# Seven of a layer's seventeen input chunks as seven block products, in a two-layer decoder trunk

## The chip, the cores and the metric

One core of a Trainium2 chip runs the whole program. The metric is the device time of one execution in microseconds (us), lower is better. The engines are PE (TensorE, matrix products), DVE (VectorE), ACT (ScalarE), POOL (GpSimd) and SP, whose queue starts the transfers. Each works through its own instructions in the order in which the program was built, and waits for others at semaphores.

## The reference

Two layers on x of 256 tokens by 2048 features, fp32. Each layer normalises, projects 2048 features to 8200 columns (q, k, v and gate of four mixers A to D of 8 heads each, and 8 forget logits), runs four kinds of causal attention, gates, projects back and adds to x:

```python
h = rms_norm(x, norm_gain[layer])
proj = jnp.einsum('bsd,dc->bsc', h, w_in[layer])       # 2048 -> 8200
qkv = proj[..., :3 * MIX_WIDTH].reshape(bsz, seq, 3, N_MIXERS, N_HEADS_PER_MIXER, HEAD_DIM)
gate = proj[..., 3 * MIX_WIDTH:4 * MIX_WIDTH]
log_f = jax.nn.log_sigmoid(proj[..., 4 * MIX_WIDTH:] + forget_bias[layer])
# A dilated windows, C block sparse, D forget-gated: softmax; B stick-breaking; A, C, D with QK-norm
y = jnp.stack([o_a, o_b, o_c, o_d], axis=1) ...
x = x + jnp.einsum('bsc,cd->bsd', y * jax.nn.silu(gate), w_out[layer])
```

## The kernel before

**Products.** Every fp32 projection is three products of a rounded format: high part by high part, high by low, low by high. The activations are split once a layer (`xh`, `xl`), the weights as they stream: a transfer on SP's queue brings `raw`, ACT copies it to the rounded `wh`, DVE subtracts to get `wl = raw - wh`, both inputs in SBUF, and PE multiplies.

**Units.** A layer has 17 input chunks of 512 columns (`IN_ORDER`, in the order qA vA kA qC vC kC, half of qD, gA, other half of qD, gC vD kD qB kB vB gD gB) and 4 output chunks. A chunk has four row blocks s of 512 features, 1 MB each, and a row block four tiles of 128 features. A unit is two such tiles, 128 x 1024 elements of weight, and `split(u + 2)` is issued just before `unit(u)`. Chunks in *token form* (q, v, k of A, C, D, and vB) hold a block of x still in PE and move 512 columns of weight past it: 96 matmuls of 512 a chunk. The others (the gates, qB, kB, and the output chunks) hold weight and move 256 tokens: 192 matmuls of 256.

**Order.** The program is built by a planner that keeps a clock for every engine from cost formulas (`Engine.cost`); each side task (evacuation of a chunk, rotary products, an attention pair of heads) is a generator that goes on when the planned clocks say its inputs are there and a buffer is free (`pe(...)`, `vs(...)`, `run_tasks`). What comes out is one fixed order for each engine. At most two pairs of heads are open at a time. A pair runs `t` (transposes of q and k), ACT's copy `qt`, `s` (scores), DVE's mask and maximum, ACT's exponentials, a scaling by 1/sum on DVE, `pt` (transposes), two copies `ptb` (one ACT, one DVE), `o`, and ACT's copy. GpSimd does the rotary products of q and k, the gains, D's mask terms, and in layer 1 the sum of squares.

**Buffers.** Three `wh`, three `wl`, three `raw` of a whole row block, five `tmp`, and two each of q, k, v, p, qt, pt and o. In PSUM four banks are for attention (`att`) and four for projections (`proj`), two to a chunk. The residual x stays in SBUF (`xt`), and so do the split outputs `yh`, `yl` of the attention. An output chunk takes its four row blocks in the order of `OUT_MIX`, A, C, D, B.

Of the kernel before, what the change touches and what calls it, by code (L numbers as in the profile page):

```python
# [11 lines left out]
F32 = mybir.dt.float32  # L12
# [5 lines left out]
P = 128  # L18
# [27 lines left out]
OUT_MIX = [A, C, D, B]  # L46
# [8 lines left out]
def units_of_layer():  # L55

    units = []
    two = [(0, 1), (2, 3)]
    for c in range(len(IN_ORDER)):
        for s in range(4):  # L60
            units += [(c, s, h) for h in ([(0, 1, 2, 3)] if halved(c) else two)]
# [47 lines left out]
class Engine:  # L109
# [39 lines left out]
    def cost(self, op, out, aps, args, kw):  # L149
# [3 lines left out]
        if self.name == "T":  # L153
# [5 lines left out]
            return max(n, 256) * 0.000425 if not four else n * 0.00169 * four  # L159
        if self.name == "S":  # L160
            return (0.19 if "accum_out" in kw else 0.1) + n * 0.00083
        if self.name == "G":
            return 0.05 + n * 0.0023
        if op == "reduce_sum":
            n = max(a.free_size() for a in aps)
        return 0.07 + n * (0.00052 if op in ("tensor_scalar_mul", "tensor_scalar") else 0.00104)
# [3 lines left out]
def hybrid_kernel(ctx, tc, x_tr, w_all, w_half, gain, qk_gain, f_bias, rope, masks, out):  # L170
# [10 lines left out]
    ATT, WB, WARM = 4, 3, 4  # L181
# [7 lines left out]
    rings["proj"] = (proj, [None] * 4)  # L189
# [4 lines left out]

    ROWS, ROW_OF = [], []
    for l, c, s, h in UNITS:
        if h[0] == 0:
            ROWS.append((l, c, s))
        ROW_OF.append(len(ROWS) - 1)

    raw, wh, wl = {}, {}, {}

    def load_raw(i):
        if i >= len(ROWS):
            return
        l, c, s = ROWS[i]
        t = new("raw", (P, 4, HW if halved(c) else CW), f"raw{i}")
        if halved(c):
            Q.dma_start(t, w_half[l, IN_ORDER[c][2], s])
            raw[i] = t  # L210
            return
        c -= sum(halved(k) for k in range(c))
        if i == 0:
            for h in range(4):
                Q.dma_start(t[:, h, :], w_all[l, c, s, :, h, :])
                if h < 2:
                    Q.dma_start(xt[0][:, h, :], x_tr[0, :, h, :])
                if h == 0:
                    Q.dma_start(gain_sb, gain)
        elif i < 3:  # L220
            for h in range(2):
# [705 lines left out]
```

## Time and profile before

| | |
|---|---|
| time, median of 3 runs | 1030.92 us (1024.12 to 1031.61) |
| profiled execution | 1027.18 us, of which its span 1025.4 us |
| mean granted clock of PE, share of full speed | 0.997 |
| busy: PE, DVE, ACT, POOL | 1006.3, 649.3, 512.2, 174.1 us |
| PE matmuls | 6772, of them 1728 of 512 columns |
| moved by DMA | 176.62 MB |

The busy time of an engine is the time in which one of its instructions ran; matmuls overlap, so that the distance from one start to the next, not the duration of one, is what a matmul costs. Times in the views count from the start of the span. In the names, what stands before the arrow is written and what stands behind it is read; an entry in square brackets is the idle time of the engine before an instruction and who ended it.

### The profile page before, as it was taken

Reading aid. Unit: us, or ns where it says so; the run is one execution under the profiler, and the core shown is the slowest. Engines: PE = TensorE matmul, PEld = TensorE weight load, DVE = VectorE, ACT = ScalarE, POOL = GpSimd, SP = SyncE. Lnnn points to the kernel's source line nnn. Section 1 sums busy time; section 2 is a strip of 40 time slices with the busy share of each in tenths; the row PEclk is TensorE's granted clock in tenths of the full one; section 3 lists DMA queues with packets and bytes.
Section 4 is the critical chain, followed back from the end, with each engine's and each line's share of the span. In section 5 each row is a group of like instructions: output and inputs, shape, how many; then the busy total and the mean of one; then the engine's idle time right before and its main releaser. Section 6 shows DMA issues by size and latency. Waiting matters only on the chain. (4 is left out here: it accounts for less than half of the span.)

```text
span 1025.4 us, 16643 instructions
## 1 busy us (share of the span) xinstructions
PE 1006.3 (98%) x6772; PEld 895.0 (87%) x6772; DVE 649.3 (63%) x1064; ACT 512.2 (50%) x791; POOL 174.1 (17%) x154
## 2 busy tenths in 40 slices
PE   8999999999998999999999999999999989999998
PEld 6887779998798899999988877899988987999998
DVE  6856757676555656757677556586765565667543
ACT  6543554656453454545454435546474444554432
POOL 0244404000045200001116044040000631000000
PEclk9999999999999999999999999999999999999999
DMA  9654435526535444555555544344465454444462
GB/s 330 235 176 165 163 121 186 179 90 217 194 125 207 162 128 160 171 197 172 201 180 203 178 151 165 123 167 166 137 225 173 145 185 158 156 144 161 165 246 83
DMA packets 30189, 176.62 MB, mean 172 GB/s; under 512 B 3984, under 2 KB 4896, under 8 KB 11040
## 3 DMA queue, kind: packets, MB, share of 16 engines
q1 hardware_dynamic: 30112, 175.55, 49.9%
q8 instruction: 53, 0.87, 0.3%
q14 instruction: 24, 0.20, 0.1%
HBM read 173.42 MB, written 2.11 MB: 171 GB/s over the span
## 5 line engine op out<-in xcount | busy, mean ns | idle before, releaser
L119 DVE TENSOR_TENSOR wl<-raw,wh 128x1024 fp32r<-128x1024 f32 (+2 forms) x321 | 411.1, 1286 | 309.4 <-ACT wh L119 307.3
L119 ACT ACTIVATE wh<-raw 128x1024 fp32r<-128x1024 f32 (+2 forms) x321 | 337.9, 1055 | 399.3 <-PE pj L119 363.1
L119 PE MATMUL pj<-wh,xh 128*128 128x512 f32 (+1 forms) x704 | 269.2, 382 | 0.5 <-ACT xh L119 0.5
L119 PE MATMUL pj<-wl,xh 128*128 128x512 f32 (+1 forms) x704 | 264.3, 375 | 1.3 <-DVE wl L119 1.3
L119 PE MATMUL pj<-wh,xl 128*128 128x512 f32 (+1 forms) x704 | 263.3, 374 | 0.0
L119 PE MATMUL pj<-xh,wl 128*128 128x256 f32 x768 | 216.8, 282 | 6.2 <-DVE wl L119 6.2
L119 PE MATMUL pj<-xh,wh 128*128 128x256 f32 x768 | 220.6, 287 | 0.0
L119 PE MATMUL pj<-xl,wh 128*128 128x256 f32 x768 | 216.5, 282 | 0.0
L119 PEld LDWEIGHTS pj<-wh,xh 128*128 128x128 f32 x704 | 132.5, 188 | 29.6 <-issue 3.4
L119 PEld LDWEIGHTS pj<-wh,xl 128*128 128x128 f32 x704 | 132.6, 188 | 26.2 <-DVE xl L119 0.2
L119 PEld LDWEIGHTS pj<-wl,xh 128*128 128x128 f32 x704 | 132.9, 189 | 25.5 <-DVE wl L119 2.4
L119 PEld LDWEIGHTS pj<-xh,wh 128*128 128x128 f32 x768 | 145.3, 189 | 8.2 <-issue 8.0
L119 PEld LDWEIGHTS pj<-xh,wl 128*128 128x128 f32 x768 | 145.4, 189 | 6.6 <-DVE wl L119 6.6
L119 PEld LDWEIGHTS pj<-xl,wh 128*128 128x128 f32 x768 | 145.2, 189 | 0.2
L119 PE MATMUL pj<-yh,wl 128*128 128x256 f32 x512 | 144.0, 281 | 0.0
L119 PE MATMUL pj<-yh,wh 128*128 128x256 f32 x512 | 143.9, 281 | 0.0
L119 PE MATMUL pj<-yl,wh 128*128 128x256 f32 x512 | 143.9, 281 | 0.0
L119 PEld LDWEIGHTS pj<-yh,wh 128*128 128x128 f32 x512 | 96.3, 188 | 0.7 <-issue 0.7
L119 PEld LDWEIGHTS pj<-yh,wl 128*128 128x128 f32 x512 | 96.5, 188 | 0.0
L119 PEld LDWEIGHTS pj<-yl,wh 128*128 128x128 f32 x512 | 96.2, 188 | 0.0
L119 ACT ACTIVATE p<-p,mx 128x128 f32<-128x128 f32 x96 | 42.2, 442 | 1.7 <-DVE mx L119 1.7
L119 POOL TENSOR_TENSOR acc<-acc,xsq 128x512 f32<-128x512 f32 x7 | 9.4, 1338 | 172.2 <-ACT xsq L119 172.0
(112 smaller groups left out, 774.9 us busy)
## 6 DMA issues: line engine op xcount, KB each, us to landing
raw<-in_w_all_dram SPq DMA_DIRECT2D x149, 1024.0 KB, 4.9
raw<-in_w_half_dram SPq DMA_DIRECT2D x16, 520.0 KB, 3.5
raw<-in_w_all_dram SPq DMA_DIRECT2D x4, 512.0 KB, 8.0
nb<-rows SPq DMA_DIRECT2D x8, 256.0 KB, 5.1
xt<-in_x_tr_dram SPq DMA_DIRECT2D x7, 256.0 KB, 7.7
out_dram<-xt SPq DMA_DIRECT2D x6, 256.0 KB, 2.2
raw<-in_w_all_dram SPq DMA_DIRECT2D x4, 256.0 KB, 3.3
mask_sb<-in_masks_dram SPq DMA_DIRECT2D x1, 512.0 KB
```

Source lines behind the costliest of these rows:

```text
L119: r = f(*args, **kw)
```

## The change

Seven chunks of a layer, q, k and v of A, k and v of D, k and v of C, are computed by Strassen's scheme in its form with seven products: tokens, features and columns are each cut in two (128 tokens, two feature tiles, 256 columns), and seven products of blocks, four banks of PSUM to a chunk, take the place of eight. Three parts are added for it. `token_forms` makes sums and differences of token blocks on GpSimd and splits them into `fh`, `fl` (ACT, DVE), once a layer. `differences` makes, for each row block of such a chunk, sums and differences of weight blocks: `da` (128 x 1024) in one GpSimd instruction and `db` in two of 128 x 512. `evac_fast` puts the products together with one ACT copy and seven DVE additions of 256 elements out of PSUM. A row block of such a chunk is four *fast units* x = 0 to 3 of 12, 12, 12 and 6 matmuls of 256 columns: x = 0 takes the left half of the raw weights, 1 and 2 the differences, and 3 a quarter of the raw ones; each has its own `wh` and `wl` (1024, 1024, 1024 and 512 elements).

The order becomes qB kB vB gB qD (both halves) gA gD qC gC, ordinary, and then the seven fast ones; of the ordinary units ten come first, then in each fast chunk four ordinary ones and after every four fast units one more, and the six left over come last. `OUT_MIX` is B, A, D, C.

To make room x leaves SBUF: layer 0 writes its new x to DRAM (`xd`, 8 writes of 256 KB), and each layer reads x back before its output chunks (`reload`, 8 reads of 256 KB a layer) into the four `xT` buffers that the differences used. `yh`, `yl` and the token forms share a ring of eight (`ys`), and a y is made only after the last fast unit (flag `dead`). PSUM is two `att` and six `proj`; there is one qt and one pt, and `raw` holds half a row block. The scaling by 1/sum and the second `ptb` copy go from DVE to ACT, layer 0's sum of squares from DVE to GpSimd, and the planner's cost formulas get other constants. ACT loads a function table 48 times in the built program, where it was 12.

```diff
 IN_ORDER = [
-    ("q", A, None), ("v", A, None), ("k", A, None),
-    ("q", C, None), ("v", C, None), ("k", C, None),
-    ("q", D, 0), ("g", A, None), ("q", D, 1), ("g", C, None), ("v", D, None), ("k", D, None),
-    ("q", B, None), ("k", B, None), ("v", B, None),
-    ("g", D, None), ("g", B, None),
+    ("q", B, None), ("k", B, None), ("v", B, None), ("g", B, None), ("q", D, 0), ("q", D, 1), ("g", A, None),
+    ("g", D, None), ("q", C, None), ("g", C, None),
+    ("q", A, None), ("k", A, None), ("v", A, None), ("k", D, None), ("v", D, None), ("k", C, None), ("v", C, None),
 ]
+FAST = 10
...
-OUT_MIX = [A, C, D, B]
+OUT_MIX = [B, A, D, C]
...
+    slow = [(c, s, h) for c in range(FAST) for s in range(4) for h in ([(0, 1, 2, 3)] if halved(c) else two)]
+    fast = [(c, s, x) for c in range(FAST, len(IN_ORDER)) for s in range(4) for x in range(4)]
+    units, slow = slow[:10], slow[10:]
+    for c in range(FAST, len(IN_ORDER)):
+        units, slow = units + slow[:4], slow[4:]
         for s in range(4):
-            units += [(c, s, h) for h in ([(0, 1, 2, 3)] if halved(c) else two)]
+            units, fast = units + fast[:4] + slow[:1], fast[4:]
+            slow = slow[1:]
+    units += slow
...
-    ATT, WB, WARM = 4, 3, 4
+    ATT, PROJ, WB, WARM = 2, 6, 3, 4
...
-    slots = dict(q=2, k=2, v=2, tmp=5, gs=4, qt=2, nb=1, p=2, be=1, pt=2, o=2, wh=WB, wl=WB, raw=3)
+    slots = dict(q=2, k=2, v=2, tmp=6, gs=4, qt=1, p=2, be=1, pt=1, o=4, wh=WB, wl=WB, raw=3, rows=2, xT=4, ys=8)
...
+            t = raw[l, c, s] = new("rows", (P, 4, CW), f"rows{u}")
+            Q.dma_start(t, w_all[l, w, s])
+            spawn(differences(l, c, s), True)
...
+    def differences(l, c, s):
+        r = raw[l, c, s]
+        yield gp(r, xT=1)
+        a = dif[l, c, s, 1] = new("xT", (P, 4, SEQ), f"da{l}_{c}_{s}")
+        av = a.rearrange("p (n j) k -> p n j k", n=2)
+        G.tensor_sub(av, r[:, :, SEQ:].rearrange("p (n j) k -> p n j k", n=2),
+                     r[:, 0:2, :].rearrange("p j (n k) -> p n j k", n=2))
+        yield gp(r, xT=1)
+        b = dif[l, c, s, 2] = new("xT", (P, 4, SEQ), f"db{l}_{c}_{s}")
+        G.tensor_sub(b[:, 0:2, :], r[:, 2:4, SEQ:], a[:, 0:2, :])
+        G.tensor_sub(b[:, 2:4, :], r[:, 2:4, 0:SEQ], b[:, 0:2, :])
...
+        G.tensor_add(g1[:, :, t1], g0[:, :, t1], g1[:, :, t1])
+        G.tensor_sub(g0[:, :, t1], g0[:, :, t0], g0[:, :, t1])
+        G.tensor_sub(g0[:, :, t0], g1[:, :, t1], g0[:, :, t0])
+        G.tensor_sub(g1[:, :, t0], g1[:, :, t0], g0[:, :, t0])
...
-        (V if l == 0 else G).tensor_add(rr["acc"], rr["acc"], sq)
...
+            G.tensor_add(rr["acc"], rr["acc"], sq)
...
+        S.activation(p1, ps[0][:, lo], AF.Copy)
+        V.tensor_add(x[:, 0, lo], ps[0][:, hi], p1)
+        V.tensor_add(t[:, 0, :], ps[2][:, lo], p1)
+        V.tensor_add(t[:, 1, :], ps[1][:, hi], t[:, 0, :])
+        V.tensor_add(x[:, 1, lo], ps[2][:, hi], t[:, 1, :])
+        V.tensor_add(x[:, 1, hi], ps[1][:, lo], t[:, 1, :])
+        V.tensor_add(t[:, 0, :], ps[1][:, lo], t[:, 0, :])
+        V.tensor_add(x[:, 0, hi], ps[3][:, lo], t[:, 0, :])
+        done(*ps, t, p1)
...
+            V.tensor_mul(o[:, 2 * b:2 * b + 2, :], gs[b], o[:, 2 * b:2 * b + 2, :])
             done(gs[b])
+        yield vs(o, ys=2)
+        yield lambda: (l, "dead") in flags and room(1e9, ys=2)
+        a = new("ys", (P, 4, SEQ), f"yh{l}{m}", F32R)
+        b = new("ys", (P, 4, SEQ), f"yl{l}{m}", F32R)
+        S.activation(a, o, AF.Copy)
+        V.tensor_sub(b, o, a)
...
-                    V.tensor_scalar_mul(p[:, i, a:b], p[:, i, a:b], de[:, 2 * i + t:2 * i + t + 1])
+                    S.activation(p[:, i, a:b], p[:, i, a:b], AF.Copy, scale=de[:, 2 * i + t:2 * i + t + 1])
...
-        V.tensor_copy(pt[:, 1, :], pt_ps[1][:, 0:384])
+        S.activation(pt[:, 1, :], pt_ps[1][:, 0:384], AF.Copy)
...
+            yield lambda: (l, "dif") in flags and room(0.0, xT=1)
+            xt[c] = new("xT", (P, 4, SEQ), f"xr{l}{c}")
+            xuses[c] = 4
+            for b in range(2):
+                Q.dma_start(xt[c][:, 2 * b:2 * b + 2, :], (x_tr if l == 0 else xd)[2 * c + b])
...
+            Q.dma_start(xd[k], xt[c][:, 2 * b:2 * b + 2, :])
...
+        for n in range(1 if x == 3 else 2):
+            o = ps[x][:, n * SEQ:(n + 1) * SEQ]
+            run_tasks()
+            for j in range(2):
+                hi, lo = {(0, 0): tok(j, t0), (0, 1): tok(2 + j, t0), (1, 0): form(2 + j, t1), (1, 1): form(j, t1),
+                          (2, 0): form(j, t0), (2, 1): tok(2 + j, t1), (3, 0): form(2 + j, t0)}[x, n]
+                w = 2 * n + j
+                first = s == 0 and j == 0 and n == 0
+                T.matmul(o, lhsT=hi, rhs=a[:, w, :], start=first, stop=False, skip_group_check=True)
+                T.matmul(o, lhsT=hi, rhs=b[:, w, :], start=False, stop=False, skip_group_check=True)
+                T.matmul(o, lhsT=lo, rhs=a[:, w, :], start=False, stop=s == 3 and j == 1, skip_group_check=True)
...
+            if s == 3:
+                flags.add((l, "dead"))
...
+        fetch(u + 16)
```

On PE, the first rows of the third chunk in the program before, which is kA of layer 0, `pj0_2`; matrix moved first behind the arrow, then what is held:

```order
L119 MATMUL pj0_2_0_577<-wh16_532,xh0_94 128x512
L119 MATMUL pj0_2_0_577<-wl16_533,xh0_94 128x512
L119 MATMUL pj0_2_0_577<-wh16_532,xl0_110 128x512
L119 MATMUL pj0_2_1_578<-wh16_532,xh0_94 128x512
L119 MATMUL pj0_2_1_578<-wl16_533,xh0_94 128x512
L119 MATMUL pj0_2_1_578<-wh16_532,xl0_110 128x512
```

The same chunk of the changed program, `pj0_11`, first unit and the start of its third, which takes a difference `da` as its weights (`wh40`) and the token form `fh00`:

```order
L126 MATMUL pj0_11_0_1194<-wh38_1145,xh0_86 128x256
L126 MATMUL pj0_11_0_1194<-wl38_1146,xh0_86 128x256
L126 MATMUL pj0_11_0_1194<-wh38_1145,xl0_94 128x256
L126 MATMUL pj0_11_0_1194<-wh38_1145,xh0_86 128x256
L126 MATMUL pj0_11_0_1194<-wl38_1146,xh0_86 128x256
L126 MATMUL pj0_11_0_1194<-wh38_1145,xl0_94 128x256
...
L126 MATMUL pj0_11_2_1196<-wh40_1190,fh00_324 128x256
L126 MATMUL pj0_11_2_1196<-wl40_1191,fh00_324 128x256
L126 MATMUL pj0_11_2_1196<-wh40_1190,fl00_325 128x256
```

Rows of 512 columns became rows of 256, twelve to a unit; the numbers 0 and 2 behind `pj0_11` are two of its four banks.

On POOL, before, what follows the tables of layer 0 is one half of the rotary products of qA:

```order
L119 TENSOR_TENSOR mq0000_561<-q000_542,tabs0_410 128x512
L119 TENSOR_TENSOR q000_542<-q000_542,tabs0_410 128x512
L119 TENSOR_TENSOR q000_542<-q000_542,mq0000_561 128x512
L119 TENSOR_TENSOR mq0001_598<-q000_542,tabs0_410 128x512
L119 TENSOR_TENSOR q000_542<-q000_542,tabs0_410 128x512
L119 TENSOR_TENSOR q000_542<-q000_542,mq0001_598 128x512
```

In the changed program, in layer 0, from the end of qA's rotary products, while the fast chunk kA (`11`) is under way:

```order
L126 TENSOR_TENSOR da0_11_2_1302<-rows48_1228 128x1024
L126 TENSOR_TENSOR db0_11_2_1328<-rows48_1228,da0_11_2_1302 128x512
L126 TENSOR_TENSOR db0_11_2_1328<-rows48_1228,db0_11_2_1328 128x512
L126 TENSOR_TENSOR da0_11_3_1388<-rows53_1316 128x1024
L126 TENSOR_TENSOR db0_11_3_1390<-rows53_1316,da0_11_3_1388 128x512
L126 TENSOR_TENSOR db0_11_3_1390<-rows53_1316,db0_11_3_1390 128x512
L126 TENSOR_TENSOR da0_12_0_1494<-rows62_1412 128x1024
L126 TENSOR_TENSOR db0_12_0_1496<-rows62_1412,da0_12_0_1494 128x512
L126 TENSOR_TENSOR db0_12_0_1496<-rows62_1412,db0_12_0_1496 128x512
```

Where POOL had rotary products alone, three instructions of differences now stand for every row block of a fast chunk, 56 row blocks in all, and rotary products between them.

On PE again, before, the step from the first to the second output chunk of layer 0 (`pj0_16` is the last input chunk, `pj0_17` the first output chunk):

```order
L119 MATMUL pj0_16_1_3884<-xh15_109,wh127_4048 128x256
L119 MATMUL pj0_16_1_3884<-xl15_125,wh127_4048 128x256
L119 MATMUL pj0_16_1_3884<-xh15_109,wl127_4049 128x256
L119 MATMUL o012_4168<-ptb012_4126,v01_3565 64x256 x2
L119 MATMUL o012_4168<-ptb012_4126,v01_3565 64x128 x2
L119 MATMUL pj0_17_0_4162<-yh0_126,wh128_4084 128x256
```

In the changed program, the first output chunk of layer 0 between its row blocks A and D, pairs of C (`02`) and D (`03`):

```order
L126 MATMUL pj0_17_1_4959<-yh00_4707,wl187_4991 128x256
L126 MATMUL t020_5098<-ident_80,q020_4575 128x128 x2
L126 MATMUL t020_5098<-ident_80,k02_4135 128x128 x2
L126 MATMUL pt0320_5104<-ident_80,p032_4547 128x128 x3
L126 MATMUL pt0321_5105<-ident_80,p032_4547 128x128 x3
L126 MATMUL o032_5115<-ptb032_5112,v03_3532 64x256 x2
L126 MATMUL o032_5115<-ptb032_5112,v03_3532 64x128 x2
L126 MATMUL s0200_5122<-qt020_5097 128x128
L126 MATMUL s0201_5123<-qt020_5097 128x128
L126 MATMUL s0200_5122<-qt020_5097 128x256
...
L126 MATMUL pt0220_5305<-ident_80,p022_5251 128x128 x3
L126 MATMUL pt0221_5306<-ident_80,p022_5251 128x128 x3
L126 MATMUL pj0_17_0_4958<-yh03_5316,wh188_5027 128x256
```

Before, at most 8 rows of attention stand between two projection rows; here there are 44 (82 matmuls) without one between `pj0_17` with the block A and with the block D, whose `yh03` needs the last pair of D. In each layer another such run of 50 matmuls stands ahead of kD.

## Rows read from the trace of the kernel before

**Rows 1.** The page: busy us (share of the span) xinstructions of each engine.

```profile
PE 1006.3 (98%) x6772; PEld 895.0 (87%) x6772; DVE 649.3 (63%) x1064; ACT 512.2 (50%) x791; POOL 174.1 (17%) x154
```

**Rows 2.** Waits: who waited for whom, us in total, times, longest us.

```profile
ACT wh L119 <- PE pj L119: 363.1, 219, 6.3
DVE wl L119 <- ACT wh L119: 307.3, 237, 5.7
...
PE pj L119 <- DVE wl L119: 7.5, 5, 3.2
```

**Rows 3.** The chain that ended last: start, us, and what.

```profile
641.87 1.51 PE s L119 x16
643.38 12.71 PE pj L119 x54
...
940.42 80.89 PE pj L119 x684
```

**Rows 4.** Windows: length, busy PE PEld DVE ACT POOL, clock, DMA share, GB/s.

```profile
300.00:325.00 25.00, 21.95 (x173) 21.28 (x172) 13.52 (x33) 9.61 (x19) 9.14 (x13) 0.93 0.54 190
400.00:425.00 25.00, 25.00 (x215) 24.55 (x214) 19.76 (x28) 12.91 (x16) 0.00 (x0) 1.00 0.49 168
800.00:825.00 25.00, 21.82 (x184) 20.69 (x184) 12.47 (x27) 10.02 (x17) 16.24 (x18) 1.00 0.35 119
```

**Rows 5.** Timeline of POOL, 114 to 123 us: start, us, instruction.

```profile
115.45 1.30 POOL L119 TENSOR_TENSOR q<-q,mq 128x512 f32<-128x512 f32 x1
116.71 1.30 POOL L119 TENSOR_TENSOR mq<-q,tabs 128x512 f32<-128x512 f32 x1
118.09 2.17 POOL L119 TENSOR_TENSOR q<-q,tabs 128x512 f32<-128x512 f32 x1
120.33 2.16 POOL L119 TENSOR_TENSOR q<-q,mq 128x512 f32<-128x512 f32 x1
```

**Rows 6.** Timeline of DVE at the same place.

```profile
116.93 4.41 DVE L119 TENSOR_TENSOR wl<-raw,wh 128x1024 fp32r<-128x1024 f32 x2 [2.71 <-ACT wh L119]
```

**Rows 7.** Timeline of DVE, 311 to 317 us.

```profile
313.39 0.42 DVE L119 CUSTOM_DVE_ANT_0 p<-s,p 128x256 f32<-128x256 f32 x1 [1.41 <-POOL p L119]
...
313.94 2.36 DVE L119 TENSOR_TENSOR wl<-raw,wh 128x1024 fp32r<-128x1024 f32 x2
316.22 1.28 DVE L119 TENSOR_TENSOR q<-pj,rb 128x512 f32<-128x512 f32 x2
```

**Rows 8.** Timeline of PE, 314 to 316 us.

```profile
315.22 0.38 PE L119 MATMUL pj<-xh,wl 128*128 128x256 f32 x1 [3.05 <-DVE wl L119]
```

**Rows 9.** Groups by line and shape: count | busy us, mean ns | idle before.

```profile
L119 DVE TENSOR_TENSOR wl<-raw,wh 128x1024 fp32r<-128x1024 f32 x303 | 389.8, 1292 | 292.8 <-ACT wh L119 290.7
...
L119 ACT ACTIVATE p<-p,mx 128x256 f32<-128x256 f32 x48 | 23.8, 495 | 0.0
L119 ACT ACTIVATE p<-p,mx 128x128 f32<-128x128 f32 x48 | 18.7, 389 | 1.7 <-DVE mx L119 1.7
...
L119 ACT ACT_TABLE_LOAD x12 | 15.4, 1283 | 0.9 <-PEq L917 0.7
L119 ACT ACTIVATE ptb<-pt 128x384 f32<-128x384 f32 x32 | 15.3, 487 | 19.6 <-PE pt L119 19.6
...
L119 ACT ACTIVATE qt<-t 128x512 f32<-128x512 f32 x24 | 13.5, 590 | 12.4 <-PE t L119 12.2
...
L119 ACT ACTIVATE o<-o 128x256 f32<-128x256 f32 x32 | 11.5, 374 | 5.5 <-PE o L119 5.0
...
L119 POOL TENSOR_TENSOR q<-q,gd 128x256 f32<-128x256 f32 x8 | 5.7, 734 | 91.0 <-DVE q L119 86.0 <-PE pj L119 5.0
```

**Rows 10.** Transfers: share of 16 engines' span; issues, KB each, us to landing.

```profile
q1 hardware_dynamic: 30112, 175.55, 49.9%
...
raw<-in_w_all_dram SPq DMA_DIRECT2D x149, 1024.0 KB, 4.9
```

More of the change, by code (lines that the diff above doesn't have):

```diff
@@ L193, in hybrid_kernel, with fast @@
     NU = len(UNITS)
[L195 to L199, printed above, removed]
-    raw, wh, wl = {}, {}, {}
-    def load_raw(i):
-        if i >= len(ROWS):
+    NI = len(IN_ORDER)
+    raw, wh, wl = {}, {}, {}
+    def fast(c):
+        return FAST <= c < NI
+    loads = {"raw": [], "rows": []}
+    for u, (l, c, s, h) in enumerate(UNITS):
+        if not fast(c):
+            loads["raw"].append(u)
+        elif h == 0:
+            loads["rows"].append(u)
@@ new lines, in free, with fetch, load @@
+    def free(tag):
+        return any(t is None or t in left for t in rings[tag][1])
+    def fetch(limit):
+        while True:
+            some = [(q[0], tag) for tag, q in loads.items() if q and q[0] < limit and free(tag)]
+            if not some:
+                return
+            u, tag = min(some)
+            loads[tag].pop(0)
+            load(u)
+    def load(u):
+        l, c, s, h = UNITS[u]
+        w = c - sum(halved(k) for k in range(c))
+        if fast(c):
+            t = raw[l, c, s] = new("rows", (P, 4, CW), f"rows{u}")
+            Q.dma_start(t, w_all[l, w, s])
+            spawn(differences(l, c, s), True)
@@ L326, in vs, with gp @@
                         and all(plan.clock.get(e, 0.0) <= plan.now() + behind[0] for e in "VS"))
+    def gp(*aps, **need):
+        names = [_tile_of(a) for a in aps]
+        return lambda: (coming(names, TOL) and room(TOL, **need)
+                        and plan.clock.get("G", 0.0) <= plan.now() + 3.0)
     def new(tag, shape, name, dtype=F32):
@@ L589, in pair @@
             if m != D:
-                yield pe(s["q"], s["k"], att=1)
+                yield pe(s["q"], s["k"], att=1, qt=1)
+            h = new("qt", (P, 2 * SEQ), f"qt{nm}")
             ps = bank(f"t{nm}")
@@ L732, in hybrid_kernel, with fast_unit, tok, form @@
     banks = {}
+    def fast_unit(u):
+        l, c, s, x = UNITS[u]
+        a, b = wh.pop(u), wl.pop(u)
+        if (l, c) not in banks:
+            while not room(1e9, proj=4):
+                advance()
+            banks[l, c] = [new("proj", (P, CW), f"pj{l}_{c}_{i}") for i in range(4)]
+        ps = banks[l, c]
+        while (l, "form", s) not in flags:
+            advance()
+        t0, t1 = slice(0, P), slice(P, SEQ)
+        fh, fl = forms[l, s, "ab"]
+        def tok(k, t):
+            return part(xh, 4 * s + k)[:, t], part(xl, 4 * s + k)[:, t]
+        def form(k, t):
+            return fh[:, k, t], fl[:, k, t]
+        for n in range(1 if x == 3 else 2):
[9 more added lines that the diff above has]
+                T.matmul(o, lhsT=lo, rhs=a[:, w, :], start=False, stop=s == 3 and j == 1, skip_group_check=True)
+        done(a, b)
+        if x == 3 and c == NI - 1:
+            done(*forms.pop((l, s, "ab")))
+            if s == 3:
+                flags.add((l, "dead"))
+        if x == 3 and s == 3:
+            kind, m, _ = IN_ORDER[c]
+            spawn(evac_fast(l, kind, m, banks.pop((l, c))), True)
+            if kind == "v":
+                spawn(attention(l, m))
     def unit(u):
@@ L785, in unit @@
         done(a, b)
+        if c == NI + 3 and h[-1] == 3:
+            done(*get(l, OUT_MIX[s])["y"])
         if s == 3 and h[-1] == 3:
```

242 lines of the change are left out of this document (150 added, 92 removed).

## The prediction

> **What bounds the kernel now.** The first view is the page's busy line: PE works in 98% of the span, DVE in 63%, ACT in 50%, POOL in 17% [rows 1]. Busy shares alone don't say who waits for whom, so the waits come next: ACT's weight copies wait 363.1 us for PE to hand a buffer back, and DVE's `wl` wait 307.3 us for ACT, while PE waits for `wl` 7.5 us in all [rows 2]. The splitters are ahead and idle; PE sets the pace. The third view is the price of PE's work, read from unbroken pieces of the chain: 54 matmuls of 512 columns took 12.71 us, 235.4 ns each, and 684 of 256 took 80.89 us, 118.3 ns each [rows 3]. A column costs the same in either form (half of 235.4 is 117.7), so nothing is lost or won by the shape, only by the count. The fourth is the windows: a typical one is full (25.00 of 25.00 at clock 1.00), and the two worst lack 3.05 and 3.18 us [rows 4]. The first of these is a lesson for the change: PE stood 3.05 us for a `wl` [rows 8], which DVE had ready only after a mask step of D that waited 1.41 us for POOL stood ahead of it [rows 7]. DVE is in order, so whatever POOL delays, delays the weights queued behind.
>
> **What the change removes.** 1344 matmuls of 512 go (14 chunks of 96) and 2352 of 256 come (14 of 168). 1344 x 0.2354 = 316.4 and 2352 x 0.1183 = 278.2: 38.1 us less. I also take off the 6.2 us of the two worst windows, which lie in stretches of D's attention that are laid out anew and priced below. 1025.4 - 38.1 - 6.2 = 981.1 us, if nothing else stands in PE's way.
>
> The Trainium skill's page "TensorE: Matmul & The Clock Gate", section "Wait — 56ns, not 53.3ns?", gives a matmul its columns at 2.4 GHz plus a fixed 2.5 ns. An estimate by it is 215.8 and 109.2 ns, a saving of 33.2 us instead of 38.1. The rows show more for both, with no fixed part that can be seen.
>
> **What it adds on the split path.** This decides. The `wl` of DVE reads two tensors from SBUF, and so do the differences of POOL, and the trace shows that these two engines don't run such instructions side by side. At 116 us POOL's products of 512 elements, 1.26 us apart while DVE waits, become 2.17 and 2.16 us long and 2.24 us apart (118.09 to 120.33) [rows 5], and two `wl` there take 4.41 us together [rows 6], where two alone take 2.36 and are 1.14 us apart (313.94 to 316.22, for two) [rows 7]. One POOL 512 and one DVE 1024 in turn need 2.24 us, against 1.26 + 1.14 = 2.40 apart: they alternate, and only 0.16 us of start-up is hidden. So beside DVE a POOL 512 costs 1.10 us. A POOL 1024 isn't in the trace; from 734 ns for 256 [rows 9] and 1.30 for 512 [rows 5], 2.2 ns an element, it is estimated at 2.4 alone, 2.24 in turn. Its bounds are 2.04 (two of 1.10 with one start-up less) and 2.6 (two of 1.30); over 26 in a stage this is -5 to +9 us. I take 2.24, which the slope gives.
>
> Now the stage from a layer's first fast unit to its last. On PE it holds 1824 matmuls of 256 (215.8 us), 192 of 512 (45.2), 192 of 260 (23.1) and some 20 us of attention: 304. On DVE what reads two SBUF tensors is 125 `wl` of 1024 at 1.14, 8 of 1040 at 1.16, 28 of 512 at 0.60 (half, and start-up), 169 us, and 25 of smaller work of the kind: 194. Another 57 us of DVE read PSUM or one tensor (the seven additions a chunk, masks, sums). On POOL in the same stage: 26 `da` x 2.24 = 58, 52 `db` x 1.10 = 57, 24 rotary products x 1.10 = 26, and 30 smaller ones (masks, gains) at about 0.55 = 16: 158 in turn. One after the other this is 194 + 158 = 352 us, against 304 of PE. The `wl` feed PE at two units' notice with three buffers, and the differences have four; neither can be made before the stage. So PE, which now waits for nobody, waits 48 us a layer at least, if these prices hold.
>
> Above this floor is the part of DVE's 57 us that doesn't fit beside a POOL instruction: all outside gives 409, half 380. DVE and POOL wait for each other in order (a split of a form behind its additions, the mask steps of D), so some is lost; but most of the 57 us is short, and POOL nearly always has an instruction to run beside it. I take three quarters hidden: 366 us, 62 more than PE's 304, for two layers 124.
>
> **What it adds in the attention.** ACT takes the scalings and second copies from DVE, and the ring of y waits for the last fast unit, so that attention of C and D comes in the run of 82 matmuls between two output row blocks, with no projection to cover it. PE's own part is 82 x 0.105 (16 scores in 1.51 us are 0.094 each [rows 3], transposes a little more) = 8.6. ACT there has 16 exponentials (8 x 0.495 + 8 x 0.389), 20 scalings (10 of 256 at 0.374 as the `o` copy, 10 of 128 at about 0.27), 10 `ptb` x 0.487, 5 `qt` x 0.590, 5 `o` x 0.374 and two copies of 1.06 [rows 9]: 25.3 us. With one `qt`, one `pt` and two `att` banks the pairs go one behind the other; bounds are 25.3 (ACT never waits) and 44 (with DVE's 10 and PE's 8.6 in turn). I take 25.3, since two pairs are open: 25.3 - 8.6 = 17 a layer, 33 for both. The run of 50 matmuls ahead of kD lies inside the fast stage, where DVE and POOL use the time; nothing is added for it, at most the 10 us a layer by which ACT's 16 exceeds PE's part.
>
> **At nothing, with the cover named.** 36 more table loads of 1.283 us [rows 9] and ACT's new work, some 180 us in all, lie under PE: ACT had 512 of 1025 busy, and in the fast stage it comes to some 226 by the prices of its rows, against 366. If ACT were the one who is late there, a load would cost its 1.3 us, 46 at most. The 6 MB of residual out and back are 3% of a traffic that takes half of the transfer engines, and row blocks land in 4.9 us [rows 10], with three half row blocks of lead (72 matmuls of 256, 8.5 us); without that cover a stall would be about that 4.9 us, once a chunk, 34 a layer. The seven additions of `evac_fast` stand ahead of `wl` on DVE; they are in the 57 us. A gain beyond the saved matmuls has a bound too: PE was idle 19.1 us of the span [rows 1], of which 6.2 are taken off already, so 13 if the new order avoids the rest.
>
> **Sum.** 981.1 + 124 + 33 = 1138, with the 1.8 us by which the profiled time exceeded its span 1140. The median shown is 1030.9, 3.7 above the profiled run; a shift of that size is in the range.
>
> **The rivals.**
> *Floor.* All of DVE's other work hides beside POOL: 352 a stage, 981.1 + 96 + 33 + 2 = 1112, and down to 1080 if attention overlaps better. For it speaks that the additions out of PSUM don't read two SBUF tensors. [...]
> *Faster.* POOL's work fits after all in what DVE leaves free: 304 - 194 = 110 us of a stage. The deciding point is whether POOL's 158 come down to 110, which they would if alternation hid 0.53 us of each of the 132 instructions (180 us alone) and not 0.16. Then PE keeps its pace: 981.1 + 33 + 2 = 1016, 983 without the attention run, 1.4 to 4.6% below before. Against it: POOL's 2.17 and 2.16 us, twice in a row, while DVE's `wl` ran.
> *Worse.* Nothing hides: 409 a stage and 44 in the attention run, 981.1 + 210 + 71 + 2 = 1264; PE with gaps may also lose its clock (0.93 in the window with the gap of 3 us [rows 4]). Against it: two engines with queues never line up so badly for 300 us.
>
> **How the numbers follow.** The forecast has 0.46 (1115 to 1185 around 1140), the floor 0.26 (1070 to 1115), worse 0.07, the fast side 0.21, of which 0.13 is over 1% faster, 0.05 within, and 0.03 a little slower. One per cent is about what a measurement of this kernel tells from no change. So faster 0.13, same 0.05, slower 0.82. The range leaves out worse above 1200 and most of the faster case below 1025: 1025 to 1200; the forecast's own is 1115 to 1185.
>
> **What would show it.** Right: matmuls of 256 still 118 ns apart inside a unit; 48 table loads; `wl` of 1024 well above their mean of 1.29 us (1.6 or more) and POOL over 400 us busy, with its instructions of 512 near 2 us where they meet `wl`; PE's wait for `wl` grown from 7.5 us to some 100; a hole of about 17 us a layer in the output chunk's middle. Wrong: PE still above 95% busy, or waits for ACT or for transfers at the place of those for `wl`; a hole that isn't in the fast stage; `da` under 2 us beside `wl`.

## The result, and the profile after

The changed kernel takes 1349.38 us (median of 4, 1341.77 to 1352.28) where the kernel before took 1030.13 in the same comparison: 1.310 times as long, with a 95% interval of 1.302 to 1.318. The prediction said slower and 1140, with a range that ended at 1200.

Its page, to be read against [rows 1]: the busy line, and the granted clock in 40 slices, in tenths.

```profile
PE 1101.4 (82%) x7780; PEld 1000.1 (74%) x7780; DVE 921.0 (68%) x1164; ACT 701.5 (52%) x1074; POOL 570.9 (42%) x361
...
PEclk8979998798889998869999998897999988896889
```

The span is 1350.5 us, so PE now idles 249 us, where it was 19. Each slice is 34 us, and 19 of the 40 lie below 0.9 (the mean is 0.903, where it was 0.997). The waits that answer to [rows 2]:

```profile
ACT wh L126 <- PE pj L126: 318.5, 204, 9.1
DVE wl L126 <- ACT wh L126: 260.5, 163, 7.6
...
PE pj L126 <- DVE wl L126: 113.3, 85, 7.3
...
PE pj L126 <- DVE q L126: 34.9, 4, 11.6
```

PE's wait for `wl` has gone from 7.5 to 113.3 us, and there is a new one, of PE's projections for a DVE result `q`, that is for an evacuation. The groups that answer to [rows 9], by shape:

```profile
L126 DVE TENSOR_TENSOR wl<-raw,wh 128x1024 fp32r<-128x1024 f32 x191 | 279.8, 1479 | 144.7 <-ACT wh L126 144.3
...
L126 POOL TENSOR_TENSOR da<-rows 128x1024 f32<-128x1024 f32 x56 | 149.5, 2670 | 245.0 <-DMA rows<-in_w_all_dram 226.0 <-DVE wl L126 11.2 <-DVE p L126 7.8
...
L126 DVE TENSOR_TENSOR wl<-db,wh 128x1024 fp32r<-128x1024 f32 x56 | 105.1, 1877 | 79.5 <-ACT wh L126 78.6
...
L126 POOL TENSOR_TENSOR db<-rows,db 128x512 f32<-128x512 f32 x56 | 99.9, 1784 | 4.4
...
L126 POOL TENSOR_TENSOR db<-rows,da 128x512 f32<-128x512 f32 x56 | 97.5, 1742 | 4.3
...
L126 ACT ACT_TABLE_LOAD x48 | 61.6, 1283 | 1.6 <-PEq L1110 0.7
```

The mean of a 1024-wide `wl` is 1.48 us on raw weights and 1.88 on `db` (it was 1.29), a `da` takes 2.67 and a `db` half 1.74 to 1.78, and the loads are 48.

**Where the time went.** From the starts of PE's matmuls, each beyond the 118 or 235 ns of its kind (and 105 ns for each attention matmul between two projections), PE's lost time can be sorted by place. Runs are places with 16 or more attention matmuls in the trace between two projections; an opening is the first matmul of a chunk; the slow clock is what is lost in steps of under 0.25 us. A step that saw only short attention, and the units of the output chunks, stand under other. Sums in us of the whole span:

| kernel | time, us | waits for wl, wh | slow clock | openings | runs | other | all |
|---|---|---|---|---|---|---|---|
| before | 1030 | 9 | 8 | 0 | 1 | 8 | 26 |
| changed | 1349 | 157 | 59 | 56 | 90 | 29 | 390 |
| e1, no differences | 1235 | 89 | 40 | 34 | 88 | 21 | 273 |
| e13, and no wl of two fast units | 1177 | 53 | 31 | 32 | 80 | 19 | 214 |
| e3, new order alone | 1192 | 13 | 8 | 39 | 118 | 13 | 191 |
| e9, e3 with four att banks | 1164 | 20 | 10 | 34 | 73 | 26 | 163 |
| e10, old order, the rest new | 1057 | 9 | 7 | 0 | 27 | 14 | 56 |

The changed kernel loses 364 us more than before, and 364 less the 38 saved in matmuls is, within 1 us, the 325 by which its span is longer. So the 38.1 us are there; all else is waiting or a slower clock, in four places of which the prediction had sized two, the waits for split weights and, too small, the runs.

Of the changed kernel's 56 us of openings 18 are of a kind of their own. Ahead of the first fast chunk PE stands for layer 0's sum of squares, with the matmul that needs it (`rb_ps`) at the head of its queue:

```profile
76.89 1.22 PE L126 MATMUL rb_ps<-xss,ones 128*128 128x256 f32 x2 [17.46 <-DVE xss L126]
```

### The profile page after: what moved, and what is told of

It is laid out like the page before. It is cut to its first block, busy times and chain, and to the rows that moved or that the text cites. A ratio compares the mean times of both kernels' runs of the same rounds, so it can differ in the third digit from the quotient of the medians.

```text
span 1350.5 us, 19797 instructions
## 1 busy us (share of the span) xinstructions
PE 1101.4 (82%) x7780; PEld 1000.1 (74%) x7780; DVE 921.0 (68%) x1164; ACT 701.5 (52%) x1074; POOL 570.9 (42%) x361
## 5 line engine op out<-in xcount | busy, mean ns | idle before, releaser
L126 DVE TENSOR_TENSOR wl<-raw,wh 128x1024 fp32r<-128x1024 f32 (+2 forms) x209 | 303.9, 1468 | 153.6 <-ACT wh L126 153.1
L126 ACT ACTIVATE wh<-raw 128x1024 fp32r<-128x1024 f32 (+2 forms) x209 | 218.6, 1053 | 262.4 <-PE pj L126 165.9
L126 PE MATMUL pj<-xh,wh 128*128 128x256 f32 x768 | 227.8, 297 | 44.5 <-DVE q L126 34.9
L126 POOL TENSOR_TENSOR da<-rows 128x1024 f32<-128x1024 f32 x56 | 149.5, 2670 | 245.0 <-DMA rows<-in_w_all_dram 226.0
L126 PE MATMUL pj<-wl,xh 128*128 128x256 f32 (+2 forms) x592 | 187.5, 317 | 20.7 <-DVE wl L126 20.7
L126 PE MATMUL pj<-wl,fh 128*128 128x256 f32 x448 | 138.8, 310 | 75.0 <-DVE wl L126 74.2
L126 PE MATMUL pj<-wh,xh 128*128 128x256 f32 (+2 forms) x592 | 187.2, 316 | 1.1 <-ACT wh L126 1.1
L126 PE MATMUL pj<-wh,xl 128*128 128x256 f32 (+2 forms) x592 | 184.5, 312 | 0.0
L126 DVE TENSOR_TENSOR wl<-rows,wh 128x1024 fp32r<-128x1024 f32 x112 | 149.3, 1333 | 15.9 <-ACT wh L126 15.8
L126 DVE TENSOR_TENSOR wl<-db,wh 128x1024 fp32r<-128x1024 f32 x56 | 105.1, 1877 | 79.5 <-ACT wh L126 78.6
L126 PE MATMUL pj<-wh,fh 128*128 128x256 f32 x448 | 134.5, 300 | 4.5 <-ACT wh L126 4.4
```

The costliest lines, as they stand in the source:

```text
L126: r = f(*args, **kw)
```

## The experiments

Each is one timed execution with its profile, beside one of the kernel before (1029.2 to 1030.3 each time). Executions of the changed kernel lie 10 us apart, so a single difference under 15 us says nothing.

**e1, the differences left out.**

```diff
-        G.tensor_sub(av, ...)                       # 1024 columns; the two of b 512 each
+        G.tensor_sub(a[:, 0, 0:8], r[:, 0, SEQ:SEQ + 8], r[:, 0, 0:8])
-                src = dif[l, c, s, h]
+                src = raw[l, c, s][:, :, SEQ:]
```

> The changed kernel with its differences left out: GpSimd's da and db instructions keep their place but cover 8 columns each instead of 1024 and 512, and the weights of the fast units 1 and 2 are split from the raw row block instead; the order on every engine is that of the changed kernel. The changed kernel took 1350 us; its two fast stages (first to last fast unit) took 449 and 440 us with 294 us of PE work in each. Theory port (DVE and GpSimd alternate at the shared port, and that sets the stage): POOL's 160 us a stage are gone, a stage falls to PE's own pace, some 310 to 340, and the whole to 1110 to 1170; wl of 1024 falls to about 1.2 us. Rival depth (three split buffers, which cover only 1.4 us of PE each in the fast units, don't bridge the attention work on DVE and ACT): the stalls stay in half or more, stages 390 or longer, the whole 1240 or more.

Measured: 1235.3 us, 114 less. The fast stage of layer 0, from the first to the last fast unit, fell from 449 to 395 us, that of layer 1 from 440 to 391: by 54 and 50, where the prediction had the port at 62 a layer above PE. The first expectation was wrong. The port is there at about its price, but 395 us is not PE's pace: the projections of the stage are 284 us and its 246 attention matmuls, at 105 ns, 26, which makes 310 (the expectations have 294). The second had the stage right and the time within 5 us; whether its cause is right, the depth of the buffers, is tested in e5 to e7.

**e13, less splitting on top of e1**: the `wl` of fast units 1 and 2 cut to 8 columns, PE reading `wh` in its place.

```diff
+            if fast(c) and h in (1, 2):
+                V.tensor_sub(b[:, 0, 0:8], src[:, 0, 0:8], a[:, 0, 0:8])
```

> As the first experiment (differences left out, 1235), and in the fast units 1 and 2 DVE's wl is cut to 8 columns, PE reading wh in its place: DVE has 112 subtractions of 1024 less, and all PE work stays. In the first experiment PE still waited 89 us for wl or wh. If it is DVE's doubled rate of splitting (a 1024-wide wl per 1.4 us of PE work where it was 2.8) that keeps PE waiting without POOL, most of the 89 us and part of the clock's 40 go: 1120 to 1165. If it is attention ahead in the queues, or ACT: 1190 or more.

Measured: 1176.8 us, 58 less than e1, and 12 above the upper end of the first expectation. PE's wait for DVE's `wl`, 113.3 us in the changed kernel, in e1 and in this one:

```profile
PE pj L127 <- DVE wl L127: 55.4, 62, 4.4
```

```profile
PE pj L127 <- DVE wl L127: 25.9, 32, 1.8
```

So the split path as a whole, differences and the second rate of `wl`, costs 114 + 58 = 172 us.

**e3, the new order alone.** No chunk in seven products; `IN_ORDER`, `OUT_MIX`, buffers, banks, spill and ACT's new work as in the changed kernel.

```diff
-FAST = 10
+FAST = 17
-            spawn(token_forms(l, c))
```

> The changed order, buffers, PSUM banks, spill and moves to ACT with no chunk in seven products: all seventeen chunks in ordinary units, no token forms, no differences. PE work is then that of the kernel before, 943 us, against 905. If what costs is the block products (port or depth): 1060 to 1110, that is 1030 plus the attention that stands uncovered before the output chunks and the later start. If what costs is the new order with two attention banks, one qt, one pt, and ACT's new work: 1180 or more.

Measured: 1192.1 us, that is 162 above the kernel before, with no Strassen in it. This is the second expectation, and the one that overturns the prediction: about half of the loss has nothing to do with block products. **e9** gives this order the attention's buffers of the kernel before, and **e10** gives the old order the rest of the change:

```diff
 e9
-    ATT, PROJ, WB, WARM = 2, 6, 3, 4        # gs=4, qt=1, pt=1
+    ATT, PROJ, WB, WARM = 4, 4, 3, 4        # gs=6, qt=2, pt=2
 e10
+IN_ORDER, OUT_MIX of the kernel before      # qt=2, pt=2
```

> The new order with no chunk in seven products, as in the third experiment (1192), with the attention's buffers of the kernel before: four att and four proj banks, two qt and two pt (and six gs for four, without which this order doesn't fit). There 118 us went in four runs of attention between projections. If the smaller buffers make those runs long, they shrink and the time is 1110 or less; if the order puts too much attention behind the last input chunk whatever its buffers, 1150 to 1195.

> The other side of the last: the order of the kernel before (IN_ORDER and OUT_MIX) with no chunk in seven products, and the rest of the change kept: two att and six proj banks, scalings and copies on ACT, the spill of x, the half row blocks, only qt and pt at two each. If the order is what costs in the third experiment, 1030 to 1080; if buffers, banks and ACT's load are, 1120 or more.

Measured: e9 1163.6 us, by its second expectation, and e10 1056.9 us, by its first. Between them lies mostly the order, 107 us (the banks differ too, four att to e9's advantage and six proj to e10's). The 28 us from e3 to e9 are the attention's buffers (with e9's six gs and four proj banks), and the 27 us from the kernel before to e10 the rest: ACT's new work, two att banks, the spill and the half row blocks; the table has 26 of them in runs. Each was one execution, so each part is known to some 10 us.

Part of what the order costs are openings, 39 us in e3 and 34 in e9, where no chunk takes four banks. In e3 PE was done with qA of layer 0 at 254 us and with gC at 232. ACT read qA for its squares, but DVE took it out of PSUM only at 411 us, and gC at 449. Four of the six banks were held that long, so that each chunk opened behind the evacuation of the one before, vA for instance behind that of kA (rows of ACT, PE and DVE in e3):

```profile
255.60 1.07 ACT L126 ACTIVATE sqq<-pj 128x512 f32<-128x512 f32 x2
...
284.26 0.76 PE L126 MATMUL pj<-wh,xh 128*128 128x512 f32 x1 [7.44 <-DVE k L126]
...
410.87 1.29 DVE L126 TENSOR_TENSOR q<-pj,ffq 128x512 f32<-128x512 f32 x2 [2.79 <-PE t L126]
...
449.44 1.28 DVE L126 TENSOR_TENSOR gs<-pj,rb 128x512 f32<-128x512 f32 x2
```

With six gs (e9) gC is evacuated at 236 us, and qA still at 404. That qA waits for one of the two q buffers is a reading of the code and wasn't tested.

What else the order does shows in the run of attention ahead of the first output chunk's D rows. Windows: length, busy PE PEld DVE ACT POOL, clock, DMA share, GB/s; of the changed kernel, the run ahead of kD, the one in the output chunk, and an opening (next section):

```profile
255.00:279.00 24.00, 15.56 (x78) 9.76 (x76) 8.94 (x36) 16.64 (x35) 0.00 (x0) 0.72 0.00 1
560.00:601.00 41.00, 26.88 (x120) 16.46 (x118) 9.02 (x46) 25.23 (x74) 5.35 (x8) 0.63 0.14 45
502.00:514.00 12.00, 0.41 (x5) 0.21 (x3) 9.69 (x14) 6.11 (x15) 7.04 (x5) 0.65 0.33 109
```

and the same place of e3:

```profile
446.90:506.90 60.00, 35.41 (x165) 21.53 (x163) 15.48 (x71) 38.92 (x110) 0.00 (x0) 0.68 0.06 19
```

No engine is full: in the 41 us PE, ACT and DVE take turns for much of the time. PE's matmuls of the changed kernel in 8 us of it:

```profile
587.28 0.44 PE L126 MATMUL t<-ident,q 128*128 128x128 f32 x2 [0.63 <-DVE mx L126]
587.56 0.38 PE L126 MATMUL t<-ident,k 128*128 128x128 f32 x2
588.69 0.93 PE L126 MATMUL s<-qt 64*128 64x128 f32 x8 [0.75 <-ACT qt L126]
591.73 1.78 PE L126 MATMUL pt<-ident,p 128*128 128x128 f32 x6 [2.11 <-ACT p L126]
594.94 1.11 PE L126 MATMUL o<-ptb,v 128*64 128x256 f32 x3 [1.44 <-ACT ptb L126]
```

The transposes `t` wait for DVE's maximum `mx`, since both att banks hold the scores of the other pair; `s` waits for ACT's copy, `pt` for ACT's scaling, `o` for ACT's copies. The clock in this stretch is 0.63. In the order before, the pairs ran between projections, and runs cost 1 us in all.

**e8, the scaling and the second copy back on DVE.**

```diff
-                    S.activation(p[:, i, a:b], p[:, i, a:b], AF.Copy, scale=de[...])
+                    V.tensor_scalar_mul(p[:, i, a:b], p[:, i, a:b], de[...])
```

> The changed kernel with the scaling by 1/sum and the second copy of a pair back on DVE, as before. If ACT's new work (about 130 us) is what makes the runs of uncovered attention long: 20 us or more less, 1330 or less. If the port and DVE's queue are what matters: DVE, which is the later engine in the fast stage, gets 50 us more, and the time rises to 1360 to 1400.

Measured: 1338.8 us, between the two expectations and within what a single run can't tell. The sum hides a trade, read as in the table above: the runs lose 55 us where it was 90, and `wl` 166 where it was 157, with a slower clock and longer short attention (62 and 21, were 59 and 13).

**e2, short scans; e4, another mix of units; e12, squares on DVE; e11, other planner costs.** Four edits of a line or two:

```diff
 e2
-                    V.tensor_tensor_scan(r, r, ones[:, 0:b - a], ...)      # r: a to b
+                    V.tensor_tensor_scan(r, r, ones[:, 0:8], ...)          # r: the last 8
 e4
-            units, fast = units + fast[:4] + slow[:1], fast[4:]
+            units, fast = units + fast[:2] + slow[:1], fast[2:]
 e12
-            G.tensor_add(rr["acc"], rr["acc"], sq)
+            (V if l == 0 else G).tensor_add(rr["acc"], rr["acc"], sq)
 e11
-            return 0.19 + n * 0.0021
+            return 0.25 + n * 0.0026        # and 1.6 for a wl
```

> The changed kernel with the stick-breaking scans of B cut from 128 and 256 columns to 8 each (so B's attention weights are not the reference's); order on every engine as in the changed kernel. The scans are the longest pieces of attention on DVE: four of them took 7.2 us in one go at 199.6 us, ahead of a wl for which PE then stood 7.3 us. Theory lumps (long attention pieces ahead of wl in DVE's queue are what two units of lead can't bridge): 8 pairs, 5 us or so of PE each in the fast stages, 1290 to 1310. Theory port: the scans take the port for 5 us a pair and no more than that, in all 30 to 40 us less; both alike there, so what tells is where it goes: by lumps the 7 us waits vanish, by port the waits of 1 to 2 us thin out everywhere.

> The changed kernel with another mix of units: after 14 ordinary ones always two fast units and one ordinary, where the changed kernel has four ordinary units at the start of each fast chunk and then one after every four fast ones. The work is the same. Rival depth: the buffers then hold about one ordinary unit (2.8 us of PE) at any time, a lead of 4.2 us in place of 2.1 to 2.8, so many short waits go: 1270 to 1310. Theory port: no work at the port is saved, and the mean over a stage is the same: 1330 to 1360.

> The changed kernel with layer 0's sum of squares back on DVE. At 59 us PE waited 17.6 us for that sum (seven additions on GpSimd, behind the tables and the first differences) with the token scale's matmul at the head of its queue. Expected: most of that wait goes, 1335 to 1342; if it only comes back as a wait for the first evacuation, 1347 to 1353.

> The changed kernel with the planner's costs at what its trace shows under the port: a wl of 1024 at 1.6 us, GpSimd at 0.25 us and 2.6 ns an element (2.9 for a da, 1.6 for 512). The work is the same; attention steps are put later in PE's queue, where the plan without the port puts them too early. If stalls come from such a plan (PE's queue held by attention that isn't ready): 1290 or less. If they come from the work itself: 1335 to 1380.

Measured: 1335.0, 1340.2, 1339.3 and 1381.6 us. The first three are 9 to 14 us below the changed kernel's median and tell little by their times. e4 and e11 came out by the second of their expectations (e11 by less than 2 us above it), e2 by neither, since both had it below 1320. e12's time lies in its first range, but not for the reason given there: the wait of 17.5 us went to 13.2.

```profile
74.57 1.22 PE L126 MATMUL rb_ps<-xss,ones 128*128 128x256 f32 x2 [13.16 <-DVE xss L126]
```

The squares still come late, since ACT makes them behind the `wh` of `da` and `db`, for which it waits on POOL (2.67 and 1.26 us). What e2 tests has its place in the trace. DVE, changed kernel, before PE's 7.3 us wait at 202 us:

```profile
199.58 7.18 DVE L126 TENSOR_TENSOR_SCAN p<-p,ones 128x128 f32<-128x128 f32 x4
...
206.81 1.82 DVE L126 TENSOR_TENSOR p<-be,p 128x768 f32<-128x768 f32 x1
208.56 1.21 DVE L126 TENSOR_TENSOR wl<-db,wh 128x1024 fp32r<-128x1024 f32 x1
```

and PE there:

```profile
202.14 0.29 PE L126 MATMUL pj<-wh,fl 128*128 128x256 f32 x1
202.27 0.28 PE L126 MATMUL pj<-wh,fh 128*128 128x256 f32 x1
209.82 0.58 PE L126 MATMUL pj<-wl,fh 128*128 128x256 f32 x1 [7.28 <-DVE wl L126]
210.20 0.41 PE L126 MATMUL pj<-wh,fl 128*128 128x256 f32 x1
210.42 0.41 PE L126 MATMUL pj<-wh,fh 128*128 128x256 f32 x1
```

Four scans took 7.18 us, `p` 1.82, and only then came the `wl` of `db`. With short scans this wait went from 7.4 to 5.1 us, since the rest of what stood ahead of it stayed. In e4 the waits for `wl` fell from 157 to 117 us and the runs from 90 to 33, but the openings rose from 56 to 120: PE's waits for evacuations grew, those for `q` from 34.9 to 50.5 us. e11 speaks against the plan's ignorance of the port as the cause of the stalls: with costs nearer to those of the trace it came out 32 us longer.

**e5 to e7, five split buffers.** For room the low parts of x are left out of the products (PE reads the high parts); e5 is the control with three buffers.

```diff
-    ATT, PROJ, WB, WARM = 2, 6, 3, 4
+    ATT, PROJ, WB, WARM = 2, 6, 5, 4        # split(u + 4), not split(u + 2); tmp=5
```

> The control for the next two: the changed kernel in which the low parts of x go to one tile and PE reads the high part of x in their place (same instructions, a wrong third product), which frees 14 KB a partition of SBUF, and with five tmp buffers for six; wh and wl stay at three buffers, split two units ahead. Expected near the changed kernel's 1350: 1330 to 1370.

> As the control (low parts of x replaced by its high parts), with five wh and five wl and splits issued four units ahead. Without the differences the changed kernel still took 1235, with 395 us in a fast stage for 294 us of PE work, so some 100 us a stage are not POOL's. Rival depth (two units of lead are 2.1 to 2.8 us of PE in the fast units, 4.2 to 5.7 in the ordinary ones): four units bridge most waits of up to 5 us; 60 us or more go, 1290 or less. Theory port alone: the port is in use 363 of 449 us; with enough lead the stage falls towards 363 plus the uncovered attention, 1230 to 1290. Neither, if dependencies of attention hold PE: 1320 or more.

> Five split buffers as in the last and the differences left out as in the first experiment. If port and depth together are the stalls of the fast stage: PE's own pace there but for the uncovered attention, 1120 to 1170. If attention (one qt, one pt, two banks, ACT's load) holds PE anyway: 1200 or more.

Measured: e5 1334.8, e6 1379.9, e7 1246.5 us. e6 and e7 came out by the last of their expectations, and the depth rival falls: 45 us longer with five buffers, and without the differences no shorter than e1 with three (1235.3, with the low parts of x in place). The fast stage of layer 0 took 436 us in e6, where e5's took 443. Yet depth did bridge what it was to bridge. Waits of e6:

```profile
PE pj L126 <- DVE q L126: 34.7, 5, 10.9
PE pj L126 <- DVE wl L126: 34.5, 24, 4.3
...
PE pj L126 <- DVE gs L126: 28.9, 6, 12.6
```

PE's wait for `wl` fell from 112.1 us in e5 to 34.5, but the splits made early stand ahead of evacuations and attention in DVE's and ACT's queues, and PE waited longer for those: by the sorting above, waits for `wl` and `wh` went from 155 (e5) to 78, openings from 52 to 106, short attention from 12 to 35, and runs from 89 to 109.

**e14, the differences on DVE.**

```diff
-        G.tensor_sub(...)                   # all three of differences
+        V.tensor_sub(...)
```

> The changed kernel with its differences on DVE in place of GpSimd; the plan's order shifts with it. By the rows a stage's work at the port falls: 26 da at 1.14 and 52 db at 0.6 are 61 us on DVE where they were 115 to 130 of POOL. If the port as a sum is what matters, 1290 to 1325. If DVE's queue is what matters (everything in order on one engine, attention behind it), 1350 or more.

Measured: 1335.0 us, between the two expectations and 14 less than the changed kernel: no more than a hint. Its groups, by shape:

```profile
L126 DVE TENSOR_TENSOR wl<-raw,wh 128x1024 fp32r<-128x1024 f32 x191 | 246.6, 1299 | 160.7 <-ACT wh L126 156.5 <-PE pj L126 3.2
...
L126 DVE TENSOR_TENSOR da<-rows 128x1024 f32<-128x1024 f32 x56 | 74.8, 1335 | 0.8 <-DMA rows<-in_w_all_dram 0.8
...
L126 DVE TENSOR_TENSOR wl<-db,wh 128x1024 fp32r<-128x1024 f32 x56 | 71.8, 1283 | 57.7 <-ACT wh L126 57.3
```

DVE does a `da` in half of POOL's time, and without the differences on POOL beside it `wl` is at 1.30 and 1.28 again; PE's waits for `wl` and `wh` fell from 157 to 107 us. But the runs of attention grew from 90 to 128, with DVE's queue fuller. The Trainium skill's "GPSIMD Engine Reference", section 4.1 "Engine selection", wants elementwise work of two inputs on VectorE, since GpSimd is some two times slower; the trace agrees (1335 against 2670 ns, the latter beside DVE's own work), and it didn't decide the kernel's time.

## Why the prediction was wrong

The step that failed is the one from prices to time: the prediction took the busiest resource, the shared port, as the length of the fast stage, priced the runs of attention by their lower bound, and had the openings and the clock at nothing. The profiled run is 212 us above the forecast. By the table some 24 of that are waits for split weights (148 more than before, predicted 124), 56 the runs (89, predicted 33), 56 the openings, 51 the slow clock and 21 other places; the 6.2 us of the two worst windows didn't come back either. Most of the signs that the prediction named came all the same (118 ns, 48 table loads, POOL busy 571 us, 113 us of waits for `wl`): they told of the port, the matmuls and the loads, and of nothing else.

**The saved matmuls, right.** 256-column matmuls still start 118 ns apart at full clock, and the ledger above closes with the 38.1 us.

**The port, nearly right.** Predicted 62 us a layer, 124 in all, for the split path; leaving the differences out gave 114, 104 of it in the two fast stages. In the fast stage of layer 0 a union of POOL's instructions and DVE's with two SBUF inputs covers some 361 us, worked out from their starts and ends, where the sum of rows was 352. That POOL's work doesn't fit, the fast rival, is out. What was wrong is the step after it: "POOL nearly always has an instruction to run", with three quarters of DVE's other work hidden, hence 366 us for the stage. It took 449 and 440. In the first of these the port was idle some 89 us, and PE had no matmul running for 89 us too, but both were idle together for only 13. So PE stood mostly while the port worked, and the port mostly while PE worked. The Trainium skill's "SBUF — State Buffer", section "Who interferes with whom", has VectorE work with two SBUF inputs contend with a GpSimd instruction that reads SBUF; the trace agrees (a `wl` from `db` takes 1.88 us where a `wl` took 1.29 before). The prediction took the slowest resource as the stage's length. The stage was longer than its busiest part, as it is when PE and its suppliers wait for each other in turn; without POOL's differences it was still 395 us for 310 of PE. That 114 came so near to 124 is in part luck: with the differences the stage was 83 us longer than predicted (449 against 366), and without them 91 longer than the 304 of PE that the prediction would have had.

**The runs of attention, mis-sized.** The sum had 17 us a layer above PE's part for the run in the output chunk, by ACT's own 25.3 us. ACT's busy time there was 25.23 us, as counted; the run lasted 41, near the 44 of the other bound, where nothing overlaps. The nearness is in part luck: that bound had PE at 8.6 us, 82 matmuls of the program at the price of one record of the trace, but an `s` or an `o` leaves two records, which makes 114 there and 12 us, and at a granted clock of 0.63 PE was busy 26.88 us. The choice between the bounds failed, with two att banks and one `qt` in plain sight. The run ahead of kD, "nothing is added for it", took 24 us, 16 beyond PE's part, where the prediction had 10 at most. Together the runs cost 90 us, not 33.

**The openings, left out.** A fast chunk needs four proj banks, an ordinary one two, and there are six. So while a fast chunk is open an ordinary one can't open until the ordinary one before it is evacuated, and the evacuation waits its turn. In the worst of these cases PE stands 11.6 us:

```profile
513.96 0.55 PE L126 MATMUL pj<-xh,wh 128*128 128x256 f32 x1 [11.59 <-DVE q L126]
```

DVE's rows there, where the evacuation of qC (`vvq` to `q`) stands behind three `wl`, two of them at 2.3 us beside POOL, and then waits for ACT's `ffq`, which itself had to load a table:

```profile
502.76 1.88 DVE L126 TENSOR_SCALAR mx<-mx 128x4 f32<-128x4 f32 x1
504.56 1.21 DVE L126 TENSOR_TENSOR wl<-raw,wh 128x1024 fp32r<-128x1024 f32 x1
505.69 2.28 DVE L126 TENSOR_TENSOR wl<-rows,wh 128x1024 fp32r<-128x1024 f32 x1
507.89 2.29 DVE L126 TENSOR_TENSOR wl<-da,wh 128x1024 fp32r<-128x1024 f32 x1
510.10 0.16 DVE L126 TENSOR_TENSOR vvq<-ssq,r 128x16 f32<-128x16 f32 x1
...
512.28 0.18 DVE L126 SCALAR_TENSOR_TENSOR faq<-ffq,vvq 128x16 f32<-128x16 f32 x1 [1.81 <-ACT ffq L126]
...
513.12 1.29 DVE L126 TENSOR_TENSOR q<-pj,ffq 128x512 f32<-128x512 f32 x2
```

ACT's table load between:

```profile
510.74 1.28 ACT L126 ACT_TABLE_LOAD   x1
```

There are four such cases, two in each layer, of some 36 us together (6.4 and 11.8 in layer 0, 6.4 and 10.9 in layer 1). With the 18 us for the sum of squares and small ones the openings are 56 us in all, at a price of nothing in the sum. Of the rows that moved the prediction followed PE's, and of PSUM it named only `att`.

**The clock, left out.** It was named in a rival and not priced. After the wait at 202 us, whose rows stand with e2, matmuls of 256 that had been 0.12 us apart start 0.22 apart (210.20, 210.42), the lower of PE's two levels (1.2 GHz against 2.4). The slow steps sum to 59 us, 8 before; how much of that would otherwise have been waiting isn't shown.

**The order as one.** What the prediction missed can be told in steps of experiments: 1030, +27 for ACT's new work, banks and spill (e10), +107 for the order (e9), +28 for the attention's buffers (e3), -15 for block products whose differences and second splits are left out (e13: 38 saved, 23 given back), +58 for those splits (e1), +114 for the differences on POOL. The prediction had 124 for the last two, which come to 172, and 33, less 6.2, for the first three, which come to 162. Each step rests on single executions some 10 us apart, so the -15 is hardly clear of nothing.

**The range.** It was built from cases of the split path and the run in the output chunk; both at their upper bound (1264) were given 7 in 100, as if each bound were a mishap. No case held a price for the openings or the clock, so that even the worst one ends 85 us below the measured time. No run beat the kernel before. Whether some other order would give the block products cover was not tried; by e13, even with most of their cost on DVE and POOL left out, this order ends 147 us above it.

## What to carry to other kernels

A stage's length is not that of its busiest engine once the engines hand small steps to each other in order; where a trace shows waits move from PE to PE's suppliers, price the chain, and take the serial bound for every stretch in which only one short chain is open. Price a change of order by what is left without cover at its end, and a change of banks by when the next user can open; test both by running the new order without the new arithmetic. Deeper buffers for one kind of work put it ahead of the others in in-order queues, so look at what it delays before counting the waits that it takes away.

## What the hardware showed

A DVE instruction of four columns can be held as long as a big one: the scale of `mx` (128 x 4) at 502.76 us, in the rows of DVE shown with the openings, took 1.88 us, while a `da` ran on POOL and ended with it:

```profile
502.21 2.41 POOL L126 TENSOR_TENSOR da<-rows 128x1024 f32<-128x1024 f32 x1
```

In the trace of the kernel before the same instruction took, with POOL idle:

```profile
313.86 0.17 DVE L119 TENSOR_SCALAR mx<-mx 128x4 f32<-128x4 f32 x1
```

In the changed kernel's trace this scale was held all six times that it started while POOL was in an instruction (0.75 to 1.91 us), and took 0.17 us the other eighteen. But not every small step is held. The reciprocal `de`, of the same 128 x 4, met POOL eight times and took 0.16 to 0.18 us each time:

```profile
482.77 0.16 DVE L126 RECIPROCAL de<-de 128x4 f32<-128x4 f32 x1
```

```profile
481.73 3.36 POOL L126 TENSOR_TENSOR da<-rows 128x1024 f32<-128x1024 f32 x1
```

So what POOL does is paid not only by wide DVE work but by some small steps of attention too, and which ones has to be read from the rows, instruction by instruction.
